# Splitting two weight blocks at a time in a two-layer hybrid transformer

## The chip, the cores and the metric

The kernel runs on one core of a Trainium2 chip. The core has a matrix engine (TensorE, PE in the profile), a vector engine (VectorE, DVE), a scalar engine (ScalarE, ACT), GpSimd (POOL) and a queue engine (SyncE, SP) that issues most of the loads. The metric is the time of one execution on the device in microseconds, as the median of several runs.

## The reference

The input is 512 tokens of width 1024 and a memory of 256 rows. There are two layers. Each one normalises its input, mixes tokens, projects with `w_out`, and adds a normalised result to the residual; then it runs a gated feed-forward of hidden width 2816. Layer 0 mixes with a chunked spatial gate, layer 1 with causal attention that has a forget gate; both also attend to the memory with four heads. Cut to what matters:

```python
for layer in range(DEPTH):
    a = rmsnorm(h, ln_mix_pre[layer])
    main = chunked_spatial_gating(...) if layer == 0 else forgetting_attention(...)
    mixed = jnp.concatenate([main, memory_attention(q_mem, mem_n, w_mem_kv[layer])], axis=-1)
    h = h + rmsnorm(mixed @ w_out[layer], ln_mix_post[layer])
    f = rmsnorm(h, ln_ffn_pre[layer])
    f = (jax.nn.silu(f @ w_ffn_gate[layer]) * (f @ w_ffn_up[layer])) @ w_ffn_down[layer]
    h = h + rmsnorm(f, ln_ffn_post[layer])
```

All inputs and outputs are float32.

## The kernel before

**Products in parts.** Each float32 operand is split into a high part, rounded to the format `fp32r`, and a low part, the remainder. A product is then three matmuls: high by high, high by low and low by high (`mm3`, lines 189 to 193). The split (`split`, line 238) is one cast on ScalarE, which makes the high part, and one subtraction on VectorE, which makes the low part; both stand in the profile under L239. Weights arrive by a load of 128 x 1024 float32 (512 KB) into a tile named `raw`, of which there are four, and are split in two halves of 128 x 512. The parts lie in tiles named `whi` and `wlo`, from two rings of eight tiles each (`pair_of_parts`, line 131). `prepared` (line 147) and `moving_pair` (line 164) load and split; with `aside` they put the parts elsewhere, among the activations.

**Feed-forward.** It takes most of the time (about 206 to 490 us for layer 0 and 780 to 1060 us for layer 1). Two hidden blocks of 128 columns are made at a time for the gate, and two for the up projection, by a scheme that replaces eight quadrant products by seven. The class `Seven` (line 1018) does this: its two raw tiles hold the quadrants a11, a12 and a21, a22, each 128 x 512. `sums` (line 1037) forms four combinations on VectorE (lines 1041, 1043, 1045, 1046), and `run` (line 1052) does one product: 12 matmuls of 128 columns of weights by 256 tokens. Products are numbered 1 to 7 and each needs one split quadrant or combination: 1 needs a11, 2 needs a12, 7 needs the combination s3, and 6, 3, 5 and 4 need what the sums have left in a11, a12, a21 and a22. Products 1, 6 and 5 share one bank, 7 and 4 another, and 2 and 3 write the two halves of a third. ScalarE copies a bank between two products that are not to be added. `sevens` (line 1088) calls them in the order 1, 7, 2, 6, 4, 3, 5, apart from the first pair of a layer, which runs 1, 2, 3 for gate and up, then (7, 6) and (4, 5) for each.

The 22 hidden blocks are worked in an opening pair and five groups of four (`groups`, line 1120). A group has four Sevens, two for the gate and two for the up projection. After each of the first four groups comes `down_sevens` (line 1238): the down projection by a seven-product scheme of its own (class `DownSeven`, line 1185) with 128 x 512 quadrants, two blocks together. There the banks of the output are `yc`, `ys` and `yl`. The hidden activations are combined and split by `Inner` (line 1158).

**Attention.** In layer 1 the heads run one after another, and the projections of keys, values and outputs are cut into pieces that are put between the steps of the heads (`attend`, line 539; `queue`, line 214). `pair_split` (line 1483) splits queries and keys of two heads.

**Order.** The program names each operation's engine. The Tile framework then orders the instructions of each engine by priority and by its own estimate of costs, gives each tile a place in its ring, and lets a place go when the last reader of the tile is done. Each engine works in its order; loads of weights wait in SP's queue until a raw tile is free.

Of the kernel before, what the change touches and what calls it, by code (L numbers as in the profile page):

```python
# [15 lines left out]
P = 128  # L16
# [24 lines left out]
def hybrid(ctx: ExitStack, tc: tile.TileContext, i: dict, out: bass.AP):  # L41
# [113 lines left out]
    def weight_parts(raw, shape, aside=False):  # L155
        n = shape[0] * shape[1]
        parts = []
        for d in range(0, n, 512):
            pair = pair_of_parts(min(512, n - d), aside)
            split(raw[:, d : min(d + 512, n)], *pair)  # L160
            parts += cut(pair, shape[1])
        return parts

    def moving_pair(src, aside=False):

        raw = wp.tile([P, 1024], F32, tag="raw", name=name("raw"), bufs=4)
        last_load[0] = nc.sync.dma_start(raw.rearrange("p (m c) -> p m c", m=4), src)
        four = raw.rearrange("p (m k c) -> p m k c", m=4, k=2)
        parts = []
        for x in range(2):  # L170
            hi, lo = (t.rearrange("p (m c) -> p m c", m=4) for t in pair_of_parts(aside=aside))
            split(four[:, :, x, :], hi, lo)
            parts.append((hi, lo))
        return parts
# [415 lines left out]
    def layer_a():  # L590
# [3 lines left out]
        wq, raws = ([], []), [wp.tile([P, 1024], F32, tag="raw", name=name("raw"), bufs=4) for _ in range(2)]  # L594

        def query_weights(m, c0, c1):
# [49 lines left out]
        with tc.tile_pool(name="sgu", bufs=1) as lp:  # L646
# [126 lines left out]
            stats()  # L773
            ws = []
            for n in range(3):
                both = wp.tile([P, 536], F32R, tag=("hi", "lo")[n % 2], name=name("ws"), bufs=8)[:, :512].rearrange(
                    "p (g x c) -> p g x c", g=2, x=2)
                split(wsf[:, 256 * n : 256 * n + 256].rearrange("p (g c) -> p g c", g=2), both[:, :, 0, :], both[:, :, 1, :])
                ws += [both[:, g, :, :] for g in range(2)]
# [238 lines left out]
    class Seven:  # L1018
# [5 lines left out]
        def __init__(self, xs, src, tag, rows):  # L1024
            self.xs, self.rows = xs, rows
            w1, w2 = loaded(src(0)), loaded(src(1))
            self.a = [w[:, d : d + 512] for w in (w1, w2) for d in (0, 512)]
            self.x, self.p = ps(tag, s="x"), ps(tag, (P, 256), s="a")
            self.q = ps(tag, (P, 256), s="e")
            self.s1, self.s2 = prob("s1"), prob("s2")  # L1030

        def parts(self, src):
            pair = pair_of_parts()
            split(src, *pair)
            return pair

        def sums(self):

            a11, a12, a21, a22 = self.a
# [5 lines left out]
            V.tensor_add(a11, a21, a11)  # L1045
            V.tensor_add(a12, a11, a12)

        def product(self, o, w, n, more=False):
# [3 lines left out]
        def run(self, what):  # L1052

            a11, a12, a21, a22 = self.a
            left, right = (slice(*c) for c in HALVES)
            s1, s2 = self.s1, self.s2
            if what == 1:
                self.product(self.p, self.w1, 0)
                A.copy(s1[:, left], self.p)
            elif what == 2:  # L1060
                self.product(self.x[:, left], self.w2, 2)
            elif what == 3:
                self.product(self.x[:, right], self.parts(a12), 5)
            elif what == 4:
                self.product(self.q, self.parts(a22), 4, True)
            elif what == 5:
                self.product(self.p, self.parts(a21), 6, True)
                A.copy(s1[:, right], self.p)
            elif what == 6:
                self.product(self.p, self.parts(a11), 3, True)  # L1070
                A.copy(s2[:, left], self.p)
            else:
                self.product(self.q, self.parts(self.s3), 1)
                A.copy(s2[:, right], self.q)
# [13 lines left out]
    def sevens(pair, plain_first, opens=False, rest=None):  # L1088

        if not plain_first:  # L1090
            for make in pair:
                u = make()
                with behind(ended if opens else ()):
                    u.sums()
                opens = False
                for n in (1, 7, 2, 6, 4, 3, 5):
                    u.run(n)
                    if rest and n == 2:
                        rest()
                        rest = None  # L1100
                u.end()
            return
# [13 lines left out]
    def feed_forward(layer, phase, xp, meanwhile=None):  # L1116
# [68 lines left out]
        class DownSeven:  # L1185

            def __init__(self, k, spare):
                if spare:
# [25 lines left out]
            def parts(self, src, aside=False):  # L1214
                pair = pair_of_parts()
                split_aside(src, *(t.rearrange("p (m c) -> p m c", m=4) for t in pair), aside)
                return pair
# [95 lines left out]
        for gi, (k0, k1) in enumerate(groups):  # L1313
            fs, pairs, downs = [], [], []
            for m in range(k0, k1, 2):
                if meanwhile and m == k1 - 2 and gi == len(groups) - 1:
                    next(meanwhile)
                if gi < len(groups) - 1:
                    pairs.append(Inner(m < k1 - 2))
                    if m > k0:  # L1320
                        downs.append(DownSeven(m, True))
                else:
# [5 lines left out]
            if gi == len(groups) - 1:  # L1328
# [3 lines left out]
                if meanwhile:  # L1332
# [7 lines left out]
                               layer == 1)  # L1340
            rest = down_sevens([DownSeven(k0, False)] + downs, pairs)


    def layer_b(phase, fp):
# [62 lines left out]
        def value_block(j):  # L1407
# [4 lines left out]
            def load():  # L1412
                for kh in range(2):
# [3 lines left out]
                    raw = loaded(i["w_v"][j, kh]).rearrange("p (a b) -> p a b", b=256)  # L1417
                    for x in range(0, 4, 2):
                        pair = [t.rearrange("p (a b) -> p a b", a=2) for t in pair_of_parts(2 * width)]
                        k = 4 * kh + x  # L1420
                        split(raw[:, x : x + 2, :], *(t[:, :, :256] for t in pair))
                        split(wf[:, k : k + 2, :], *(t[:, :, 256:] for t in pair))
                        w.extend(tuple(t[:, y, :] for t in pair) for y in range(2))

# [217 lines left out]
```

## Time and profile before

| what | value |
|---|---|
| median of 3 runs | 1090.25 us (1089.44 to 1091.18) |
| profiled execution | 1089.34 us |
| its span, first to last instruction | 1087.6 us |
| mean granted TensorE clock | 0.999 |
| TensorE busy | 1079.2 us, 7266 matmuls |
| weight loads busy (PEld) | 982.4 us |
| VectorE busy | 971.8 us, 1942 instructions |
| ScalarE busy | 755.9 us, 1588 instructions |
| GpSimd busy | 93.5 us, 120 instructions |

A row of a group names the line, the engine, the operation, the tiles (out<-in) and the shapes, then the count, the busy time in us and the mean of one in ns, and after the second bar the idle time before them and what ended it. A row of a wait reads "engine tile line <- releaser: us in total, times, longest". A row of the timeline has the start and the length in us. Matmuls overlap, so their rows are longer than the distance between two starts.

### The profile page before, as it was taken

The page shows a single profiled execution, that of the slowest core. Times are in us where ns is not written, and L with a number is a line of the kernel's source. Part 1 is how long each engine was busy: PE and PEld are TensorE (multiplying, and loading weights), DVE is VectorE, ACT ScalarE, POOL GpSimd, SP SyncE. Part 2 cuts the span into 40 slices and gives each one's busy share as a digit, 9 for nine tenths or more (in the row PEclk, how much of TensorE's full clock was granted, in tenths as well). Part 3 has the DMA queues.
Part 4 walks back from the last instruction along what each step waited for, and adds up shares of the span by engine and source line. Part 5 has one row for each costly group of instructions (what it writes and reads, how often), then busy time and mean ns, then how long its engine had stood idle before and what let it go on. Part 6 is the DMA issues. An engine that isn't in the chain of part 4 may idle for free.

```text
span 1087.6 us, 19810 instructions
## 1 busy us (share of the span) xinstructions
PE 1079.2 (99%) x7266; PEld 982.4 (90%) x7267; DVE 971.8 (89%) x1942; ACT 755.9 (69%) x1588; POOL 93.5 (9%) x120
## 2 busy tenths in 40 slices
PE   9999999999999999999999999999999999999998
PEld 8998889998989898998988998889997989898996
DVE  7879768999999999997968789868999999999986
ACT  7776578667766667577747788868666666757664
POOL 1000000002020202001000000000002010201100
PEclk9999999999999999999999999999999999999999
DMA  7421441338464664746222654531347465564632
GB/s 272 161 83 42 121 130 39 117 97 194 128 156 129 144 182 97 195 145 187 78 78 61 156 135 125 151 117 40 99 116 173 119 154 158 120 193 94 177 97 78
DMA packets 83993, 139.65 MB, mean 128 GB/s; under 512 B 6772, under 2 KB 49800, under 8 KB 83896
## 3 DMA queue, kind: packets, MB, share of 16 engines
q1 hardware_dynamic: 71480, 116.57, 34.9%
q0 software_dynamic: 11712, 21.50, 11.6%
q8 instruction: 57, 0.93, 0.4%
q10 hardware_dynamic: 704, 0.32, 0.1%
q14 instruction: 40, 0.33, 0.1%
HBM read 105.23 MB, written 2.10 MB: 99 GB/s over the span
## 4 chain that ended last, share of the span: by engine, by line
PE 71%; DVE 19%; DMA 4%; issue 3%; ACT 3%; SPq 0%; DVEq 0%; ACTq 0%
DVE wlo L239 6%; PE y L191 5%; PE y L192 5%; PE y L193 5%; PE ps L191 4%; PE ps L193 4%; PE ps L192 4%; DMA raw<-in_w_gate 4%; PE a L191 3%; PE a L192 3%; PE a L193 2%; PE v L191 2%; PE yc L191 2%; PE v L192 2%; PE v L193 2%
## 5 line engine op out<-in xcount | busy, mean ns | idle before, releaser
L239 ACT CAST whi<-raw 128x512 fp32r<-128x512 f32 x444 | 264.0, 620 | 100.7 <-DVE raw L1045 27.4
L239 DVE TENSOR_TENSOR wlo<-raw,whi 128x512 fp32r<-128x512 f32 x444 | 292.5, 687 | 22.1 <-ACT whi L239 21.2
L191 PE MATMUL x<-xshi,whi 128*128 128x256 f32 x320 | 90.0, 281 | 0.0
L193 PE MATMUL x<-xshi,wlo 128*128 128x256 f32 x320 | 90.0, 281 | 0.0
L191 PE MATMUL a<-xshi,whi 128*128 128x256 f32 x320 | 90.0, 281 | 0.0
L192 PE MATMUL x<-xslo,whi 128*128 128x256 f32 x320 | 89.9, 281 | 0.0
L192 PE MATMUL a<-xslo,whi 128*128 128x256 f32 x320 | 89.8, 281 | 0.0
L193 PE MATMUL a<-xshi,wlo 128*128 128x256 f32 x320 | 89.8, 281 | 0.0
L191 PE MATMUL ps<-xshi,whi 128*128 128x256 f32 (+1 forms) x224 | 68.5, 306 | 0.0
L192 PE MATMUL ps<-xslo,whi 128*128 128x256 f32 (+1 forms) x224 | 66.7, 298 | 0.0
L193 PE MATMUL ps<-xshi,wlo 128*128 128x256 f32 (+1 forms) x224 | 66.4, 298 | 0.0
L239 ACT CAST whi<-s 128x512 fp32r<-128x512 f32 x56 | 34.8, 621 | 38.8 <-DVE s L1208 18.6
L192 PEld LDWEIGHTS a<-xslo,whi 128*128 128x128 f32 x320 | 60.3, 189 | 0.4
L191 PEld LDWEIGHTS a<-xshi,whi 128*128 128x128 f32 x320 | 60.3, 188 | 0.4
L193 PEld LDWEIGHTS x<-xshi,wlo 128*128 128x128 f32 x320 | 60.4, 189 | 0.0
L192 PEld LDWEIGHTS x<-xslo,whi 128*128 128x128 f32 x320 | 60.3, 189 | 0.0
L193 PEld LDWEIGHTS a<-xshi,wlo 128*128 128x128 f32 x320 | 60.3, 189 | 0.0
L191 PEld LDWEIGHTS x<-xshi,whi 128*128 128x128 f32 x320 | 60.3, 188 | 0.0
L1243 POOL DMA_DIRECT2D y<-yo x48 | 41.4, 953 | 192.2 <-ACT yo L1242 130.8
L191 PE MATMUL y<-whi,mixedhi 128*128 128x512 f32 x128 | 51.4, 401 | 0.0
L192 PE MATMUL y<-wlo,mixedhi 128*128 128x512 f32 x128 | 50.7, 396 | 0.0
L193 PE MATMUL y<-whi,mixedlo 128*128 128x512 f32 x128 | 50.4, 394 | 0.0
(353 smaller groups left out, 3656.3 us busy)
## 6 DMA issues: line engine op xcount, KB each, us to landing
raw<-in_w_gate SPq DMA_DIRECT2D x44, 512.0 KB, 4.5
raw<-in_w_up SPq DMA_DIRECT2D x44, 512.0 KB, 5.7
y<-yo POOLq DMA_DIRECT2D x64, 256.0 KB, 4.9
raw<-in_w_down SPq DMA_DIRECT2D x28, 512.0 KB, 4.1
raw<-in_w_out SPq DMA_DIRECT2D x16, 512.0 KB, 4.0
wd<-in_w_down SPq DMA_DIRECT2D x32, 256.0 KB
flo<-s POOLq DMA_DIRECT2D x16, 256.0 KB, 4.8
raw<-in_w_b_q SPq DMA_DIRECT2D x8, 512.0 KB, 4.4
```

The costliest lines, as they stand in the source:

```text
L191: PE.matmul(o, w[0], x[0], start=start, stop=False, skip_group_check=more)
L192: PE.matmul(o, w[0], x[1], start=False, stop=False, skip_group_check=more)
L193: return PE.matmul(o, w[1], x[0], start=False, stop=stop, skip_group_check=more)
L239: last_parts[:] = A.copy(hi, src), (eng or V).tensor_sub(lo, src, hi)
L1243: G.dma_start(ys[to[0]][to[1]], some, accum_op=ALU.add)
```

## The change

Two neighbouring blocks of 512 columns are cast and subtracted together, as one of 1024, and the rings have four tiles of 1072 columns where they had eight of 512 (536 for one block). `prepared` and `moving_pair` split a whole raw tile at once. In `Seven`, the quadrants are split as (1, 2), (6, 3), (5, 4) and 7 alone, and the order of the products becomes 1, 2, 7, 6, 3, 4, 5, which puts the two halves of each wide tile next to each other; the pair (6, 3) is split when the first of its products is due. Where two blocks are not neighbours, only the tile is shared and the splits stay 512 wide: the query weights of layer 0, the quadrants of the down products (through the new class `Halves`), and queries and keys in `pair_split`. The spatial weights of layer 0 take three halves of one pair of wide tiles.

```diff
-    def pair_of_parts(n=512, aside=False):
-        if aside:
-            return act("whi"), act("wlo")
-        return (wp.tile([P, max(n, 512)], F32R, tag="hi", name=name("whi"), bufs=8)[:, :n],
-                wp.tile([P, max(n, 512)], F32R, tag="lo", name=name("wlo"), bufs=8)[:, :n])
+    def pair_of_parts(n=1024):
+        return tuple(wp.tile([P, 1072], F32R, tag=t, name=name("w" + t), bufs=4)[:, :n] for t in ("hi", "lo"))
+
+    class Halves:
+
+        def __init__(self):
+            self.left = []
+
+        def __call__(self):
+            if not self.left:
+                self.left = cut(pair_of_parts(), 512)
+            return self.left.pop(0)
...
     def weight_parts(raw, shape, aside=False):
         n = shape[0] * shape[1]
+        step = 512 if aside else n
         parts = []
-        for d in range(0, n, 512):
-            pair = pair_of_parts(min(512, n - d), aside)
-            split(raw[:, d : min(d + 512, n)], *pair)
+        for d in range(0, n, step):
+            pair = (act("whi"), act("wlo")) if aside else pair_of_parts(n)
+            split(raw[:, d : d + step], *pair)
             parts += cut(pair, shape[1])
         return parts
...
+        if not aside:
+            pair = pair_of_parts()
+            split(raw, *pair)
+            hi, lo = (t.rearrange("p (m k c) -> p m k c", m=4, k=2) for t in pair)
+            return [(hi[:, :, x, :], lo[:, :, x, :]) for x in range(2)]
...
-        def parts(self, src):
-            pair = pair_of_parts()
-            split(src, *pair)
-            return pair
+        def parts(self, *ns):
+            pair = pair_of_parts(512 * len(ns))
+            split(self.raw[ns], *pair)
+            self.w.update(zip(ns, cut(pair, 512)))
 
         def sums(self):
 
             a11, a12, a21, a22 = self.a
-            self.s3 = temp("s3")
-            V.tensor_add(self.s3, a11, a21)
-            self.w1 = self.parts(a11)
+            s3 = temp("s3")
+            self.w, self.raw = {}, {(1, 2): self.raws[0], (6, 3): self.raws[0], (5, 4): self.raws[1], (7,): s3}
+            V.tensor_add(s3, a11, a21)
+            self.parts(1, 2)
             V.tensor_add(a21, a21, a22)
-            self.w2 = self.parts(a12)
             V.tensor_add(a11, a21, a11)
             V.tensor_add(a12, a11, a12)
+
+        def weights(self, n):
+            if n not in self.w:
+                self.parts(*next(ns for ns in self.raw if n in ns))
+            return self.w[n]
...
-                for n in (1, 7, 2, 6, 4, 3, 5):
+                for n in (1, 2, 7, 6, 3, 4, 5):
                     u.run(n)
-                    if rest and n == 2:
+                    if rest and n == 7:
...
             def parts(self, src, aside=False):
-                pair = pair_of_parts()
+                pair = self.halves()
...
-            pair["q"], pair["k"] = pair_of_parts(), pair_of_parts()
+            pair["q"], pair["k"] = cut(pair_of_parts(), 512)
```

More of the change, by code (lines that the diff above doesn't have):

```diff
@@ L168, in moving_pair @@
         four = raw.rearrange("p (m k c) -> p m k c", m=4, k=2)
+        if not aside:
[3 more added lines that the diff above has]
+            return [(hi[:, :, x, :], lo[:, :, x, :]) for x in range(2)]
         parts = []
         for x in range(2):
-            hi, lo = (t.rearrange("p (m c) -> p m c", m=4) for t in pair_of_parts(aside=aside))
+            hi, lo = (act(t).rearrange("p (m c) -> p m c", m=4) for t in ("whi", "wlo"))
             split(four[:, :, x, :], hi, lo)
@@ L594, in layer_a @@
         wq, raws = ([], []), [wp.tile([P, 1024], F32, tag="raw", name=name("raw"), bufs=4) for _ in range(2)]
+        query_parts = [pair_of_parts() for _ in range(2)]
         def query_weights(m, c0, c1):
@@ L598, in query_weights @@
             for c in range(c0, c1, 512):
-                pair = pair_of_parts()
+                pair = tuple(t[:, c : c + 512] for t in query_parts[m])
                 split(raws[m][:, c : c + 512], *pair)
@@ L774, in layer_a @@
             ws = []
+            hi, lo = pair_of_parts()
+            room = hi[:, :512], lo[:, :512], hi[:, 512:]
             for n in range(3):
-                both = wp.tile([P, 536], F32R, tag=("hi", "lo")[n % 2], name=name("ws"), bufs=8)[:, :512].rearrange(
-                    "p (g x c) -> p g x c", g=2, x=2)
+                both = room[n].rearrange("p (g x c) -> p g x c", g=2, x=2)
                 split(wsf[:, 256 * n : 256 * n + 256].rearrange("p (g c) -> p g c", g=2), both[:, :, 0, :], both[:, :, 1, :])
@@ L1052, in run @@
         def run(self, what):
-            a11, a12, a21, a22 = self.a
             left, right = (slice(*c) for c in HALVES)
@@ L1057, in run @@
             if what == 1:
-                self.product(self.p, self.w1, 0)
+                self.product(self.p, self.weights(1), 0)
                 A.copy(s1[:, left], self.p)
             elif what == 2:
-                self.product(self.x[:, left], self.w2, 2)
+                self.product(self.x[:, left], self.weights(2), 2)
             elif what == 3:
-                self.product(self.x[:, right], self.parts(a12), 5)
+                self.product(self.x[:, right], self.weights(3), 5)
             elif what == 4:
-                self.product(self.q, self.parts(a22), 4, True)
+                self.product(self.q, self.weights(4), 4, True)
             elif what == 5:
-                self.product(self.p, self.parts(a21), 6, True)
+                self.product(self.p, self.weights(5), 6, True)
                 A.copy(s1[:, right], self.p)
             elif what == 6:
-                self.product(self.p, self.parts(a11), 3, True)
+                self.product(self.p, self.weights(6), 3, True)
                 A.copy(s2[:, left], self.p)
             else:
-                self.product(self.q, self.parts(self.s3), 1)
+                self.product(self.q, self.weights(7), 1)
                 A.copy(s2[:, right], self.q)
@@ L1185, in feed_forward, with __init__ @@
         class DownSeven:
-            def __init__(self, k, spare):
+            def __init__(self, k, spare, halves):
+                self.halves = halves
                 if spare:
@@ L1313, in feed_forward @@
         for gi, (k0, k1) in enumerate(groups):
-            fs, pairs, downs = [], [], []
+            fs, pairs, downs, halves = [], [], [], Halves()
             for m in range(k0, k1, 2):
@@ L1320, in feed_forward @@
                     if m > k0:
-                        downs.append(DownSeven(m, True))
+                        downs.append(DownSeven(m, True, halves))
                 else:
@@ L1417, in load @@
                     raw = loaded(i["w_v"][j, kh]).rearrange("p (a b) -> p a b", b=256)
[L1418 to L1423, printed above, removed]
+                    pair = [t.rearrange("p (a b) -> p a b", a=4) for t in pair_of_parts(4 * width)]
+                    split(raw, *(t[:, :, :256] for t in pair))
+                    split(wf[:, 4 * kh : 4 * kh + 4, :], *(t[:, :, 256:] for t in pair))
+                    w.extend(tuple(t[:, y, :] for t in pair) for y in range(4))
             def piece(tk, kh):
```

6 lines of the change are left out of this document (3 added, 3 removed).

## The prediction

> **What bounds the kernel now.** I began with the profile's page: the busy time of each engine, and the forty slices.
>
> ```profile
> span 1087.6 us, 19810 instructions
> PE 1079.2 (99%) x7266; PEld 982.4 (90%) x7267; DVE 971.8 (89%) x1942; ACT 755.9 (69%) x1588; POOL 93.5 (9%) x120
> DVE  7879768999999999997968789868999999999986
> PEclk9999999999999999999999999999999999999999
> ```
>
> TensorE is busy in 1079.2 of 1087.6 us and its clock is never lowered. VectorE stands at 90% or more in two long blocks of slices, which are the two feed-forward layers. The next view is the busy time by stage: the feed-forward of layer 0 with its four down products, a stretch of three Sevens alone, the attention of layer 1, and the feed-forward of layer 1. Columns: length, then PE, PEld, DVE, ACT and POOL busy with their instruction counts, the granted clock, the DMA share and GB/s.
>
> ```profile
> 206.00:441.00 235.00, 234.29 (x1641) 216.12 (x1640) 231.24 (x414) 159.54 (x319) 33.22 (x38) 1.00 0.58 146
> 441.90:471.70 29.80, 29.80 (x252) 29.75 (x251) 29.77 (x55) 19.19 (x42) 1.72 (x2) 1.00 0.53 156
> 580.00:720.00 140.00, 139.36 (x836) 120.54 (x835) 116.51 (x317) 111.17 (x273) 0.00 (x0) 1.00 0.48 125
> 780.00:1011.00 231.00, 229.69 (x1622) 212.22 (x1621) 227.97 (x408) 157.14 (x316) 32.79 (x38) 1.00 0.57 143
> ```
>
> In the three Sevens, TensorE starts 252 matmuls in 29.80 us, one every 0.118 us without a hole, while VectorE is just as full: 29.77 of 29.80 us. Both are full at once, so I have to find out which one makes the other wait. The lead tells it: the part that product 7 reads, and the moment at which product 7 reads it.
>
> ```profile
> 448.98 0.69 DVE L239 TENSOR_TENSOR wlo<-s,whi 128x512 fp32r<-128x512 f32 x1
> 453.50 0.28 PE L191 MATMUL e<-t3hi,whi 128*128 128x256 f32 x1
> ```
>
> The low part is done at 448.98 + 0.69 = 449.67, and product 7 starts at 453.50: 3.8 us ahead, or 2.7 products (a product is 12 matmuls, 12 x 0.118 = 1.42 us). So TensorE sets the pace inside the Sevens and VectorE keeps up with some stock. Where does TensorE wait at all? First the list of its waits over the whole run, then the eight stretches in which the down products of a group run.
>
> ```profile
> PE idle L89 <- DVE zeros L81: 1.3, 1, 1.3
> PE ys L193 <- DVE flo L239: 0.6, 3, 0.2
> PE yc L191 <- ACT yo L1242: 0.5, 3, 0.2
> PE ys L191 <- DVE s L1080: 0.4, 1, 0.4
> 241.40:262.48 21.08, 20.73 (x86) 1.00 0.65 134
> 302.26:322.33 20.07, 19.98 (x86) 1.00 0.67 137
> 362.06:382.09 20.03, 19.96 (x87) 1.00 0.66 136
> 421.98:442.13 20.15, 19.95 (x86) 1.00 0.66 140
> 815.09:836.58 21.49, 20.78 (x87) 1.00 0.64 131
> 876.29:896.36 20.07, 19.96 (x86) 1.00 0.67 137
> 936.02:956.15 20.13, 19.98 (x86) 1.00 0.68 139
> 995.83:1016.30 20.47, 20.14 (x87) 1.00 0.61 128
> ```
>
> The waits shown are tiny, but a matmul row is longer than the distance between two starts, so a late start hides under the end of the one before. The starts themselves say more:
>
> ```profile
> 818.54 0.40 PE L191 MATMUL yl<-whi,fhi 128*128 128x512 f32 x1
> 819.70 0.40 PE L193 MATMUL yl<-whi,flo 128*128 128x512 f32 x1
> 816.97 0.39 PE L193 MATMUL ys<-whi,flo 128*128 128x512 f32 x1
> 817.74 0.50 PE L191 MATMUL ys<-whi,fhi 128*128 128x512 f32 x1 [0.38 <-DVE s L1080]
> 824.22 0.40 PE L192 MATMUL ys<-wlo,fhi 128*128 128x512 f32 x1
> 824.85 0.50 PE L193 MATMUL ys<-whi,flo 128*128 128x512 f32 x1 [0.23 <-DVE flo L239]
> ```
>
> From 818.54 to 819.70 lie five steps, 0.232 us each. A down stretch is 7 products x 2 blocks x 2 token blocks x 3 = 84 matmuls, 84 x 0.232 = 19.49 us (the counts of 86 and 87 take in neighbours that overlap the edges). The eight stretches sum to 163.49 us, their floor to 155.92: 7.6 us are lost there, and hardly anything in the Sevens. The two starts shown are 0.77 - 0.23 = 0.54 and 0.63 - 0.23 = 0.40 us late, both behind VectorE. Those 7.6 us are the most that these stretches can give back.
>
> **The change, part by part.** *Merged splits.* A split is one ACT cast and one DVE subtraction. The groups of the splits, and the same operations at half the width, priced by form:
>
> ```profile
> L239 DVE TENSOR_TENSOR wlo<-raw,whi 128x512 fp32r<-128x512 f32 x444 | 292.5, 687 | 22.1 <-ACT whi L239 21.2
> L239 ACT CAST whi<-raw 128x512 fp32r<-128x512 f32 x444 | 264.0, 620 | 100.7 <-DVE raw L1045 27.4 <-PE a L192 24.6 <-PE ps L192 14.8
> L239 DVE TENSOR_TENSOR b<-s,b 128x256 fp32r<-128x256 f32 x16 | 6.8, 422 | 0.2 <-ACT b L239 0.2
> L239 ACT CAST b<-s 128x256 fp32r<-128x256 f32 x16 | 6.5, 405 | 0.6 <-ACT fhi L239 0.3
> 450.51 2.49 DVE L239 TENSOR_TENSOR wlo<-raw,whi 128x512 fp32r<-128x512 f32 x4
> 449.10 1.14 ACT L239 CAST whi<-raw 128x512 fp32r<-128x512 f32 x2 [0.71 <-DVE raw L1045]
> ```
>
> No row shows a split of 1024, so I carry the line on. DVE: 256 more elements cost 687 - 422 = 265 ns, so 1024 take 687 + 530 = 1217 ns. Four in a row took 2.49 us, so starts are (2.49 - 0.69) / 3 = 0.60 us apart and 87 ns of each overlap the next. A merged subtraction occupies 1217 - 87 = 1130 ns where two occupied 1200: 70 ns less. The bounds are 0 (no fixed part) and 157 ns (687 - 530, all of the fixed part); I take 70, because the spacing is what a full engine feels. ACT: 620 - 405 = 215 per 256, so 1050 ns; spacing 1.14 - 0.62 = 0.52; merged 950 against 1040: 90 ns less, bounds 0 and 190.
>
> How many? Each of the 40 Sevens goes from 7 splits to 4, so 120 merges. The other 62 are counted in the code: memory keys and values 8, first projection 12, first blocks of the three boundaries 6, first down weights 4, output weights 8, unaside tail weights 8, layer-1 queries 4, keys 6, values 6. The small forget columns merge twice more. The three kinds that only share a tile (query weights, q/k pair, down quadrants through Halves) keep 512-wide splits. VectorE loses 182 x 70 ns = 12.7 us of work, ScalarE 182 x 90 ns = 16.4 us. Inside the Sevens all of it lies beside matmuls that start every 0.118 us anyway: cost and gain there are 0. Were that cover gone, a Seven would gain 3 x 70 = 0.21 us of its 9.93.
>
> *What reaches the end.* A group has four Sevens, 12 merges, 0.84 us less VectorE work before its down products. The waits behind VectorE at these stretches (the low part of the hidden activations, and the sums of line 1080) should shrink by up to that. From the two starts above, 0.54 + 0.40 us, and the smaller late starts in the other six (those six lose 0.54 to 0.98 us each, of which the copies of the chain banks by ACT, line 1242, take about half), I put the part owed to VectorE at 2.5 us of the 7.6. The chain-bank copies wait for TensorE itself and stay. Bounds 0 and 7.6; I take 1.5, the row of the three visible low-part waits being nearest: **-1.5 us**.
>
> *Later first use.* The first product of a pair now waits for a cast and a subtraction of double width: 1050 - 620 + 1217 - 687 = 0.96 us later if both start when they did. The 3.8 us of lead hide that; where no lead is left it costs up to 0.96 us each time.
>
> *The order 1, 2, 7, 6, 3, 4, 5.* It lets the halves of a pair be used one behind the other. Product 2 writes a bank of its own; 7 still has 6 and 3 between it and the product 4 that adds to its bank, 6 has 2 and 7 between it and product 1. So no product moves closer to the copy that empties its bank than two products, 2.8 us against copies of 0.36 us: 0. The cast of (6, 3) has to wait for both sums, lines 1045 and 1046, not for the first alone; they precede product 6 by a product and more: 0. The raw tiles are let go after the subtractions of (6, 3) and (5, 4); SP's loads are queued behind that, and the first of the two is earlier than before, where product 3 split last but one: 0, bounds -0.3 and +0.3 us per layer.
>
> *Four slots of 1072 for eight of 512.* Bytes are the same, but a slot is let go only when both halves are read. The rows of ACT waiting for a slot, and of the loads behind the splits:
>
> ```profile
> ACT whi L239 <- PE a L192: 24.6, 40, 0.8
> SPq L144 <- DVE wlo L239: 256.2, 66, 27.1
> ```
>
> Already one cast per Seven (40 times, 0.6 us on average) waits until TensorE has read an old high part, so the ring is full once a Seven. With four slots TensorE holds one pair and five products' worth can lie ready: 5 x 1.42 = 7.1 us between a slot's release and its next need, against 1.05 + 1.22 = 2.3 us to fill it, plus what stands ahead on VectorE. That hides it: 0; the price without this cover is in the rivals.
>
> *Attention of layer 1.* 32 of its splits become 16:
>
> ```profile
> L239 DVE TENSOR_TENSOR wlo<-raw,whi 128x512 fp32r<-128x512 f32 x32 | 21.5, 685 | 1.9 <-ACT whi L239 1.7
> ```
>
> VectorE is busy in 116.51 of 140 us there and ScalarE in 111.17, so nothing is gained by less work as such; a softmax step that finds a merged subtraction ahead of it can be 0.53 us later. Bounds: 16 x 0.07 = -1.1 and 16 x 0.53 = +8.5 us. Projection matmuls stand ready to fill such holes (TensorE shows 0.64 us idle in 140), so I take **+0.3 us**.
>
> The sum goes against the profiled execution's own time, 1089.34 us, which is 1.74 over its span: 1089.34 - 1.5 + 0.3 = 1088.1. That execution lies 0.9 below the median of the runs, 1090.25, so the forecast for the median is **1089.0 us**: no change that can be told from none, 0.2% (2.2 us) being about what a measurement of this kernel tells.
>
> **The rivals.** *A: VectorE's relief goes further.* If its lag at the end of each group is what holds the down stretches, half or more of the 7.6 us goes: 1090.25 - 4 = 1086.2, with everything 1082.7. For it: both stretches with the most loss (21.08, 21.49) follow the first groups, where VectorE must also finish the inputs. Against it: five of eight lose only 0.5 to 0.7 us.
>
> *B: the coarser ring makes TensorE wait (slower).* Place: where a group's down products begin. Slots there are shared between the last pair of the Sevens and the first two down quadrants, and one tile holds the quadrants 1 and 7, taken long before 7 is multiplied. If a free slot appears one product late, filling it takes 2.3 us and the product in hand covers 1.4: 0.9 us per stretch, 8 x 0.9 = 7.2, less the 1.5: 1090.25 + 5.7 = 1096. It decides once VectorE's lead there is under about 1 us. For it: ACT's 40 waits on the ring. Against it: they are at most 0.8 us and TensorE never waited in answer.
> The Trainium skill, Perfetto Trace Analysis, section Identifying Performance Opportunities, says that the same gap repeating on the engine that should be saturated can mean that there was no room for the next tile; this trace has such a gap on ACT (24.6 us in 40), not on TensorE.
>
> *C: long instructions stand in the way in attention (slower).* If a third of the 16 merged subtractions hold back a step that TensorE needs, 5.3 x 0.53 = 2.8 us: 1090.25 + 2.8 = 1093. For it: neither VectorE (83%) nor ScalarE (79%) is full there. Against it: the 0.64 us of idle.
> The Trainium skill, Perfetto Trace Analysis, section Optimizing Scalar/DVE Operations, recommends grouping where such an engine is saturated, and breaking instructions up where it isn't but makes others wait; by that rule the change is right in the Sevens and wrong here.
>
> **How the numbers follow.** Forecast 0.47, A 0.28, B 0.12, C 0.13. The forecast's own range is 1087.7 to 1091.5, so a little of it falls under 1088.07: faster 0.30, same 0.45, slower 0.25. The range runs from 1085.5 (most of A) to 1094.0 (all of C, little of B), which also holds the -1.1 of attention with half of A.
>
> **What would show it.** Right: merged casts near 1050 and subtractions near 1217 ns, 182 of each; VectorE's busy time down by 12 to 19 us with TensorE's start spacing still 0.118; the two longest down stretches below 20.7 us. Wrong: waits of TensorE behind the low parts inside the Sevens (B), a down stretch above 21.5, or more than 0.64 us of TensorE idle between 580 and 720 (C).

## The result and the profile after

The changed kernel takes 1105.17 us, the median of six runs (1100.90 to 1108.80); the kernel before, run beside it, takes 1090.61 us (1089.44 to 1091.53). The ratio is 1.0135, with a 95% interval of 1.0110 to 1.0161. The change makes the kernel **slower by 14.6 us**. The forecast was 1089.0 us and the range ended at 1094.0, so the forecast and its range were wrong.

The page of the changed kernel, its span and the engines' busy time. The profiled execution took 1104.32 us:

```profile
span 1102.6 us, 19371 instructions
PE 1081.0 (98%) x7266; PEld 979.1 (89%) x7267; DVE 963.1 (87%) x1758; ACT 734.4 (67%) x1404; POOL 93.8 (9%) x120
```

TensorE has the same 7266 matmuls, at the same clock (0.999). VectorE has lost 8.7 us of work and ScalarE 21.5 us, as the change means them to. The span has grown by 15.0 us all the same. Where do they lie? The eight stretches of the down products, with the same columns as in the prediction:

```profile
244.21:264.70 20.49, 19.99 (x86) 1.00 0.61 123
304.61:326.72 22.11, 20.61 (x86) 1.00 0.62 127
366.06:388.21 22.15, 20.64 (x87) 1.00 0.62 128
427.70:449.29 21.59, 20.66 (x86) 1.00 0.61 129
827.96:848.45 20.49, 19.98 (x86) 1.00 0.61 125
...
sum 171.35, PE 163.66; mean PE 20.46
```

They sum to 171.35 us where they were 163.49: 7.9 us more. The change isn't even. The first stretch of each layer became shorter (21.08 to 20.49 and 21.49 to 20.49, 1.6 us together), and the other six grew by 9.5 us. Line numbers have moved: the split, L239 before, is L252; the first and last sums of a Seven, L1041 and L1046, are L1059 and L1063; the sum L1080 at the end of a Seven is L1101.

To place the rest I took all starts of TensorE in the trace and summed by how much each is late, that is, the distance from the start before it less 0.117 us (256 columns) or 0.230 us (512):

| late starts of TensorE, us | before | after |
|---|---|---|
| Sevens of each layer's first group | 0.8 | 5.5 |
| Sevens of layer 0's last group | 0.4 | 2.4 |
| Sevens of the other groups | 2.9 | 1.4 |
| down products | 8.8 | 16.8 |
| everything else, attention included | 30.6 | 32.2 |

So 13.2 of the 15 us are lost in the feed-forwards, at three places: in the first group of a layer, in the last group of layer 0, and where a group's down products run. The 1.5 us by which the other Sevens differ are 0.6 ns on each of their 2352 starts: in the Sevens of the kernel before no single start is over 0.02 us late, so this is a spacing and not a wait that went away. Why TensorE is late at the three places begins on VectorE. Groups of VectorE and ScalarE instructions, by form:

```profile
L252 DVE TENSOR_TENSOR wlo<-raw,whi 128x1024 fp32r<-128x1024 f32 x182 | 219.3, 1219 | 17.4 <-ACT whi L252 17.0
L252 ACT CAST whi<-raw 128x1024 fp32r<-128x1024 f32 x182 | 189.5, 1048 | 128.2 <-DVE raw L1063 57.7 <-PE x L205 19.2 <-issue 9.7
L1059 DVE TENSOR_TENSOR s<-raw,raw 128x512 f32<-128x512 f32 x40 | 27.4, 686 | 16.6 <-DMA raw<-in_w_gate 15.7 <-DMA raw<-in_w_up 0.8
```

The merged instructions cost what was forecast. But the first sum of a Seven now finds VectorE idle for 16.6 us in all, because its quadrants have not been loaded; before, it was 1.7 us. One such case, followed through the timeline of the changed kernel (start, length, instruction, and in brackets the idle time before it and what ended it):

```profile
264.88 2.00 ACT L252 CAST whi<-raw 128x1024 fp32r<-128x1024 f32 x2 [3.98 <-PE yc L206]
266.51 2.35 DVE L252 TENSOR_TENSOR wlo<-raw,whi 128x1024 fp32r<-128x1024 f32 x2
267.75 1.47 SPq L151 DMA_DIRECT2D raw<-in_w_gate  x2
272.43 0.69 DVE L1063 TENSOR_TENSOR raw<-raw 128x512 f32<-128x512 f32 x1
275.48 0.69 DVE L1059 TENSOR_TENSOR s<-raw,raw 128x512 f32<-128x512 f32 x1 [2.36 <-DMA raw<-in_w_gate]
...
307.47 0.41 DVE L1101 TENSOR_TENSOR s<-a,s 128x256 f32<-128x256 f32 x1
306.48 0.40 PE L206 MATMUL ys<-whi,flo 128*128 128x512 f32 x1
307.94 0.50 PE L204 MATMUL ys<-whi,fhi 128*128 128x512 f32 x1 [1.06 <-DVE s L1101]
```

Read it from the top. ScalarE waits 3.98 us for a place for the parts, until a down product (`yc`) has let one go. The two wide casts then run, the two wide subtractions end at 267.73 and 268.86, and each time SP can issue a load into the raw tile that is free at last. The second of these loads lands some 6.6 us after its issue. VectorE, which works in its fixed order, runs out of work at 273.12 and stands idle until 275.48. From there to 307.88 no idle time is shown on it; the sum at 307.47, which frees a bank for `ys`, comes at the end of that unbroken row, and TensorE's next matmul starts 307.94 - 306.48 - 0.23 = 1.2 us late behind it. That the hole is what made the sum late is read from this order; the runs below put it to the test. The same happens at 213.86, where the hole is 2.61 us long and VectorE then has none until product 6 stalls:

```profile
213.86 0.69 DVE L1059 TENSOR_TENSOR s<-raw,raw 128x512 f32<-128x512 f32 x1 [2.61 <-DMA raw<-in_w_gate]
...
235.90 0.68 DVE L1063 TENSOR_TENSOR raw<-raw 128x512 f32<-128x512 f32 x1
236.61 1.04 ACT L252 CAST whi<-raw 128x1024 fp32r<-128x1024 f32 x1
236.39 0.28 PE L206 MATMUL e<-t3hi,wlo 128*128 128x256 f32 x1
237.71 0.39 PE L204 MATMUL a<-d2hi,whi 128*128 128x256 f32 x1 [1.03 <-ACT whi L252]
```

The last sum of that Seven ends at 236.58, the wide cast of (6, 3) starts at 236.61, and product 6, which could have started at 236.51, starts at 237.71. The twin of this start in layer 1, at 821.43, is 1.27 us late.

The casts show what holds the parts back. First the waits of ScalarE in the kernel before, then after (in all, times, longest):

```profile
ACT whi L239 <- DVE raw L1045: 27.4, 27, 1.8
ACT whi L239 <- PE a L192: 24.6, 40, 0.8
ACT whi L239 <- PE x L192: 6.6, 13, 0.6
```

```profile
ACT whi L252 <- DVE raw L1063: 57.7, 27, 3.5
ACT whi L252 <- PE x L205: 19.6, 24, 1.0
ACT whi L252 <- PE a L205: 11.0, 14, 1.3
ACT whi L252 <- PE yc L206: 8.0, 2, 4.0
```

The wait for the sums has doubled. The waits for a place (those on PE) are fewer but longer: up to 4.0 us, where in the feed-forwards none was above 0.8.

### The profile page after: what moved, and what is told of

Same layout as the page of the kernel before. It is cut to its first block, busy times and chain, and to the rows that moved or that the text cites. A ratio compares the mean times of both kernels' runs of the same rounds, so it can differ in the third digit from the quotient of the medians.

```text
span 1102.6 us, 19371 instructions
## 1 busy us (share of the span) xinstructions
PE 1081.0 (98%) x7266; PEld 979.1 (89%) x7267; DVE 963.1 (87%) x1758; ACT 734.4 (67%) x1404; POOL 93.8 (9%) x120
## 4 chain that ended last, share of the span: by engine, by line
PE 67%; DVE 22%; ACT 4%; issue 3%; DMA 3%; SPq 0%; DVEq 0%; ACTq 0%
DVE wlo L252 8%; PE y L205 4%; PE y L206 4%; PE y L204 4%; PE ps L204 4%; PE ps L206 4%; PE ps L205 4%; DMA raw<-in_w_gate 2%; PE a L204 2%; PE a L205 2%; PE a L206 2%; PE v L204 2%; PE v L206 2%; PE v L205 2%; PE yc L204 2%
## 5 line engine op out<-in xcount | busy, mean ns | idle before, releaser
L252 ACT CAST whi<-raw 128x1024 fp32r<-128x1024 f32 (+1 forms) x262 | 237.2, 917 | 138.1 <-DVE raw L1063 57.7
L252 DVE TENSOR_TENSOR wlo<-raw,whi 128x1024 fp32r<-128x1024 f32 (+1 forms) x262 | 272.8, 1056 | 22.6 <-ACT whi L252 21.9
L204 PE MATMUL a<-d2hi,whi 128*128 128x256 f32 x160 | 45.3, 283 | 2.1 <-ACT whi L252 2.1
```

Source lines behind the costliest of these rows:

```text
L204: PE.matmul(o, w[0], x[0], start=start, stop=False, skip_group_check=more)
L252: last_parts[:] = A.copy(hi, src), (eng or V).tensor_sub(lo, src, hi)
```

## The experiments

Two theories ran against each other. The **places**: four wide places for the parts are fewer and coarser than eight narrow ones, so casts wait for a place. The **merged splits**: a wide cast of (6, 3) waits for the last sum, and a raw tile is let go only after a wide subtraction, so sums, loads and the work behind them come late. Beside them stood the **order** of the products. Every kernel computes the whole reference. "Idle behind loads" is VectorE's idle time before the first sums; "FFN late" is the sum of late starts in Sevens and down products, 12.9 us before and 26.1 after.

### The order of the products alone

The kernel before, with the new order and nothing else:

```diff
-                for n in (1, 7, 2, 6, 4, 3, 5):
+                for n in (1, 2, 7, 6, 3, 4, 5):
-                    if rest and n == 2:
+                    if rest and n == 7:
```

> The kernel before with nothing but the order of the products changed to 1, 2, 7, 6, 3, 4, 5; 512-wide splits, rings of eight. Both theories: the order by itself is neutral, 1088 to 1093. A third theory, that the order is what hurts: 1098 or more.

Measured: 1092.63 us, 1.0023 (1.0013 to 1.0034). FFN late is 15.3 us and idle behind loads 5.6 us. The order costs about 2.5 us, a sixth of the loss.

### Fewer narrow places

The kernel before, with its two rings cut from eight tiles to seven and to six:

```diff
-        return (wp.tile([P, max(n, 512)], F32R, tag="hi", name=name("whi"), bufs=8)[:, :n],
-                wp.tile([P, max(n, 512)], F32R, tag="lo", name=name("wlo"), bufs=8)[:, :n])
+        return (wp.tile([P, max(n, 512)], F32R, tag="hi", name=name("whi"), bufs=6)[:, :n],
+                wp.tile([P, max(n, 512)], F32R, tag="lo", name=name("wlo"), bufs=6)[:, :n])
```

> The kernel before, with rings of seven tiles of 512 in place of eight; nothing else. In the wide ring of the changed kernel a Seven's four tiles hold 7 x 512 useful columns, since product 7 fills half of one. Theory 2 (too few places for parts): 1094 to 1105, TensorE late at the down products as in the changed kernel. Theory 1 (the merged split itself): one place less is nothing, 1089 to 1092.

> The kernel before, with rings of six tiles of 512. Theory 2: more than with seven, 1100 to 1115; a wide slot is let go one product (1.4 us) later than a narrow one, which is about another place. Theory 1: 1089 to 1094.

Measured: 1093.09 us with seven (1.0033; 1.0020 to 1.0046), between the two theories' ranges, and 1100.53 us with six (1.0100; 1.0084 to 1.0116), in the range of the places. A wait of ScalarE with six:

```profile
ACT whi L239 <- PE a L192: 39.6, 62, 2.0
```

62 waits up to 2.0 us where there were 40 up to 0.8. Losing two narrow places costs 10.9 us with nothing else changed: the ring had almost no stock to give away. FFN late goes from 12.9 to 25.0 us, above all in the down products (8.8 to 17.1), as in the changed kernel (16.8).

### The merged splits undone, in the changed kernel

`halves` keeps the wide tiles and splits each half of a Seven's pair when its product is due. `apart63` does that for (6, 3) alone.

```diff
-        def parts(self, *ns):
-            pair = pair_of_parts(512 * len(ns))
-            split(self.raw[ns], *pair)
-            self.w.update(zip(ns, cut(pair, 512)))
+        def parts(self, n):
+            ns = next(ns for ns in self.raw if n in ns)
+            if n not in self.room:
+                pair = pair_of_parts(512 * len(ns))
+                self.room.update(zip(ns, cut(pair, 512)))
+                if ns not in ((1, 2), (6, 3), (5, 4)):
+                    split(self.raw[ns], *pair)
+                    self.w.update(zip(ns, cut(pair, 512)))
+            if n not in self.w:
+                at = 512 * ns.index(n)
+                split(self.raw[ns][:, at : at + 512], *self.room[n])
+                self.w[n] = self.room[n]
```

> The changed kernel, but in the Sevens each product's 512 columns are cast and subtracted by themselves when that product is due, into the wide tiles; new order, ring of four and the merged splits outside the Sevens stay. Theory 1 (the merged split is what hurts: the cast of (6, 3) has to wait for the last of the three sums, and raw tiles are let go late behind that): 1090 to 1093 us, VectorE idle at the first sum behind loads down from 16.6 us to under 5. Theory 2 (the ring of four wide tiles is what hurts, a slot being let go only when both halves are read): stays at 1101 to 1109, with the same idle time behind loads.

> The changed kernel, but of the Seven's pairs only (6, 3) is split in two halves of 512, each when its product is due; (1, 2) and (5, 4) stay merged. Theory 1, in its narrow form (the wait of one cast for both sums): most of the 14.6 us comes back, 1091 to 1095, and the late starts of product 6 behind ScalarE's cast (1.2 us each) are gone. Theory 2: no change, 1101 to 1109.

Measured: `halves` 1102.59 us (1.0108; 1.0087 to 1.0129), `apart63` 1106.92 us (1.0151; 1.0132 to 1.0171). In `halves` the wait for the last sums shrinks, and the wait for a place grows:

```profile
ACT whi L252 <- PE x L205: 36.4, 38, 1.0
ACT whi L252 <- PE a L205: 16.0, 15, 2.0
ACT whi L252 <- DVE raw L1072: 12.0, 23, 2.0
```

On four wide places the merged splits are therefore not what costs the 14.6 us: without them 12.5 remain. Splitting (6, 3) alone gains nothing.

The kernel to set beside `halves` is the one with the order alone. Both split each half of a pair by itself, in the same order of products, so they differ by the wide places and by the wide splits outside the Sevens: 1092.63 to 1102.59 us, 10.0 us, and FFN late goes from 15.3 to 24.1 us.

### The sums first

The changed kernel, with its three in-place sums at high priority:

```diff
+            with tc.high_priority():
-            V.tensor_add(a21, a21, a22)
-            V.tensor_add(a11, a21, a11)
-            V.tensor_add(a12, a11, a12)
+                V.tensor_add(a21, a21, a22)
+                V.tensor_add(a11, a21, a11)
+                V.tensor_add(a12, a11, a12)
```

> The changed kernel, with the three sums in the raw tiles raised in priority, so that VectorE does them as soon as their operands are there; splits, ring and order stay. Theory 1: the cast of (6, 3) and the raw tiles come earlier and half or more of the loss goes, 1092 to 1098. Theory 2: 1101 to 1109, as the slots are no freer.

Measured: 1101.11 us (1.0101; 1.0086 to 1.0116), about 4 us better than the change; idle behind loads stays at 15.5 us. Late sums alone are not the cause.

### The pairing without the wide tiles

The kernel before with the new order, its eight narrow places and its 512-wide splits, but both halves of a pair split together when the first is due:

```diff
+        def weights(self, n):
+            if n not in self.w:
+                ns = next(ns for ns in self.src if n in ns)
+                self.w.update(zip(ns, [self.parts(src) for src in self.src[ns]]))
+            return self.w[n]
```

> The kernel before in the new order, with narrow tiles, rings of eight and 512-wide splits, but both splits of a pair, (1, 2), (6, 3) and (5, 4), are called together when the first of them is due. If it is the pairing that hurts (two places claimed at once, the raw tile let go later, both sums needed first): 1097 or more, and VectorE idle at the first sum behind loads above 10 us. If pairing costs nothing with narrow tiles: 1091 to 1094, as with the order alone, and what hurts is the width of the instruction and of the place.

Measured: 1096.12 us (1.0061; 1.0046 to 1.0076), 3.5 us over the order alone and between the two ranges. ScalarE's wait for the sums is as long as in the changed kernel:

```profile
ACT whi L239 <- DVE raw L1045: 56.4, 34, 2.4
```

but with eight narrow places it costs little. The kernels so far take 1090.6 us before, 1092.6 with the order, 1096.1 with the pairs split together in narrow tiles, 1102.6 in `halves` and 1105.2 with everything. These are not the steps of one stair, as `halves` has the wide places but takes the pairing back.

### Product 7 in tiles of its own

The changed kernel, where product 7's parts don't take half a wide place but a pair of 512-wide tiles of their own (one pair). To make room, the masks and the small forget tiles move to the pool of layer 1's attention. `own7_sums` adds the high priority for the sums.

```diff
-            pair = pair_of_parts(512 * len(ns))
+            pair = pair_of_parts(1024) if len(ns) > 1 else tuple(
+                seven_pool[0].tile([P, T], F32R, tag=f"w7{t}", name=name("w" + t), bufs=1) for t in ("hi", "lo"))
```

> The changed kernel, but the parts of product 7 lie in a pair of 512-wide tiles of their own, so that the four wide slots serve only the pairs (1, 2), (6, 3), (5, 4) and the down quadrants. To make room, the masks and small tiles of layer 1's attention are kept in that layer's own pool. Theory 2: a third or more of a slot's time is free again, and most of the loss goes, 1091 to 1097. Theory 1: 1100 to 1107 as before, with product 6 still late behind its cast.

> As the kernel with product 7's parts in tiles of their own, and the three sums raised in priority. If both causes add: 1088 to 1093, and less than with either alone. If only the ring counts: the same as with the tiles alone.

Measured: 1115.92 us (1.0241; 1.0224 to 1.0259) and 1115.76 us (1.0237; 1.0221 to 1.0252): both worse than the change, a miss. A new wait of TensorE appears in the first of them:

```profile
PE e L212 <- ACT s L1105: 5.5, 5, 1.6
```

Product 4 waits for ScalarE to empty its bank. But moving the masks is an edit too (the next control), so this pair doesn't separate the theories.

### Five wide places, and the splits merged or not

Five places need room. The rings go into pools that live for one stage (4 x 1072 outside the feed-forwards), and small tiles move out. So there is a control, `ring4s`, with the same pools and four wide places of 1024 in the feed-forwards. Four kernels make a square: four or five places, merged or halved splits (halved as in `halves`).

```diff
+    with tc.tile_pool(name="ffn0", bufs=4) as xp, ring_of("ring_f0", 1024, 4):
...
-    with tc.tile_pool(name="ffn0", bufs=4) as xp, ring_of("ring_f0", 1024, 4):
+    with tc.tile_pool(name="ffn0", bufs=4) as xp, ring_of("ring_f0", 1024, 5):
...
-    last_ring = ctx.enter_context(ring_of("ring_f1", 1024, 4))
+    last_ring = ctx.enter_context(ring_of("ring_f1", 1024, 5))
```

> A control: the changed kernel with its wide rings in pools that live for one stage each (four places of 1024 in the feed-forwards, four of 1072 elsewhere), and with the masks and small tiles of layer 1 in that layer's pool. Nothing in the feed-forward's work differs. Every theory: 1100 to 1110, as the changed kernel; anything else is the price of moving tiles.

> As the control, with five wide places in the feed-forwards in place of four; all splits merged as in the changed kernel. Theory 2 (too few places): most of the loss goes, 1090 to 1096. Theory 1 (the merged split delays the first half and the raw tiles): 1100 or more.

> Five wide places, and in the Sevens 512-wide splits, each when its product is due. Theory 2: 1090 to 1094, no better than with merged splits. If the ring and the merged split both cost: this is the one near 1091, and the merged one with five places lies between.

> The control with pools of one stage, four wide places, and 512-wide splits in the Sevens. With five places the same kernel took 1098.1 and its late starts in the feed-forwards were those of the kernel before. If the fifth place is what did that: 1106 to 1110 here, with late starts in Sevens and down products together near 24 us. If the 512-wide splits did it alone: 1097 to 1100.

Measured, in us, with the ratio to the kernel before and its interval, and FFN late:

| | splits merged | splits halved |
|---|---|---|
| four places | 1112.27, 1.0213 (1.0196 to 1.0230), late 28.0 | 1114.02, 1.0217 (1.0200 to 1.0234), late 27.9 |
| five places | 1113.42, 1.0218 (1.0178 to 1.0258), late 26.9 | 1098.10, 1.0077 (1.0062 to 1.0092), late 13.0 |

Either remedy alone gives nothing; both together give 14 to 16 us, and bring FFN late to 13.0 us, where the kernel before has 12.9. With the fifth place alone the late starts only move, from the Sevens (15.1 to 10.5 us) to the down products (12.9 to 16.4). The casts' waits shift too. Four places merged, five places merged, four places halved, five places halved (L1081 and L1090 are the last sums, L1089 the one before):

```profile
ACT whi L269 <- DVE raw L1081: 55.7, 26, 3.4
ACT whi L269 <- PE x L222: 22.8, 27, 1.0
ACT whi L269 <- PE a L222: 18.4, 22, 1.7
```

```profile
ACT whi L269 <- DVE raw L1081: 72.5, 29, 3.9
ACT whi L269 <- PE x L222: 7.3, 9, 1.0
```

```profile
ACT whi L269 <- PE x L222: 37.6, 39, 1.0
ACT whi L269 <- PE a L222: 27.0, 22, 2.0
ACT whi L269 <- DVE raw L1090: 9.3, 22, 0.9
```

```profile
ACT whi L269 <- DVE raw L1089: 26.3, 23, 2.1
ACT whi L269 <- PE a L222: 19.0, 20, 1.2
ACT whi L269 <- PE x L222: 18.4, 25, 1.0
```

A fifth place takes most of the waits for a place away, and the wait for the sums rises to 72.5 us. Halved splits take the wait for the sums away, and those for a place rise. Only with both does the kernel come back to about the waits of the kernel before. There VectorE never waits for a load, and the down stretches are shorter than ever:

```profile
L1085 DVE TENSOR_TENSOR s<-raw,raw 128x512 f32<-128x512 f32 x40 | 27.5, 688 | 0.0
```

```profile
sum 161.26, PE 160.73; mean PE 20.09
```

161.26 us against 163.49 before. This kernel is still slower than the one before, because its late starts outside the feed-forwards are 40.1 us, like those of its control (38.2), and not 30.6.

### Five raw tiles, and the sums first on five places

`raw5s` is the control with a fifth raw tile in the feed-forwards; for that its raw tiles, too, lie in pools that live for one stage. `ring5_sums` is `ring5` with the sums at high priority (that diff stands above).

```diff
-    with tc.tile_pool(name="ffn0", bufs=4) as xp, ring_of("ring_f0", 1024, 4):
+    with tc.tile_pool(name="ffn0", bufs=4) as xp, ring_of("ring_f0", 1024, 4, 5):
```

> The control with five raw tiles in the feed-forwards in place of four, and four wide places. If the loss comes from VectorE idling at the first sum behind late loads (16.6 us of idle in the changed kernel): 1092 to 1098. If the places for parts are what runs out: 1099 or more, with the idle at the first sum gone all the same.

> Five wide places, merged splits, and the three sums raised in priority. If with five places the merged split hurts because its cast waits for sums that VectorE does late: 1100 to 1106, late starts near 15 us. If it hurts because raw tiles, and with them the loads and the first sum, come late: 1110 or more, with VectorE still idle some 15 to 20 us at the first sum.

Measured: `raw5s` 1123.37 us (1.0306; 1.0291 to 1.0322), `ring5_sums` 1115.34 us (1.0223; 1.0199 to 1.0248). With the fifth raw tile VectorE's idle time behind loads falls from 15.7 to 1.3 us:

```profile
L1077 DVE TENSOR_TENSOR s<-raw,raw 128x512 f32<-128x512 f32 x40 | 27.5, 688 | 1.3 <-DMA raw<-in_w_up 0.7 <-DMA raw<-in_w_gate 0.5
```

FFN late falls only from 28.0 to 21.5 us: a load that comes late accounts for a part, and the rest stays. It is the Sevens that gain (15.1 to 8.8 us). The down products stay at 12.9 and 12.7; only the two late starts behind the sum that frees `ys`, 1.1 us together in the control, are gone. The time as a whole gets worse because the late starts outside the feed-forwards rise to 55.0 us. The trace shows where: at each change of stage. One of three:

```profile
506.94 0.38 SPq L192 DMA_DIRECT2D raw<-in_w_down  x1
512.07 0.79 PE L221 MATMUL y<-whi,fhi 128*128 128x512 f32 x1 [5.17 <-ACT whi L269]
```

The last matmul of the stage before ends at 506.91, SP then issues the first load into the new stage's raw tiles, and TensorE starts again 5.3 us late, when that block has come and been split. The other two, at 146.49 and 741.57, are 4.9 us late each. The control is 4.0 us late at these three starts, so they make 11.1 of the 16.8 us by which 55.0 exceeds its 38.2. So this run prices the late loads in the feed-forwards, but its total says nothing about a fifth raw tile as such.

Putting the sums first doesn't help on five places either, where idle behind loads is 23.0 us.

## Why the prediction was wrong

**Prices: right.** 182 merged subtractions of 1219 ns and 182 casts of 1048 ns were measured where 1217 and 1050 were forecast. TensorE's spacing is unchanged. VectorE's busy time fell by 8.7 us, below the 12 to 19 named as the sign: 48 ns per merge where 70 were taken, inside the bounds of 0 and 157. Back to back, two wide subtractions start 2.35 - 1.22 = 1.13 us apart, which is the forecast spacing. ScalarE's busy time fell by 21.5 us, 118 ns per merge where 90 were taken.

**"-1.5 us" at the down stretches: wrong in sign.** They grew by 7.9 us. The two longest did fall below 20.7 us, which was named as a sign of being right, and the 1.6 us are what the term forecast; but both follow the first groups, where TensorE had by then lost 2.3 and 2.4 us more than before, so VectorE may only have caught up. The other six grew, four of them past the 21.5 named as a sign of being wrong. The Trainium skill, Perfetto Trace Analysis, section Optimizing Scalar/DVE Operations, says that grouping can improve throughput where such an engine is saturated. VectorE was that in the Sevens, and the grouping did lower its work, but it had idle time behind loads (16.6 us in all) where it had little before, and no throughput was gained: in the steady Sevens TensorE set the pace already.

**"Four slots of 1072 for eight of 512: 0": wrong, the first of two main errors.** The argument counted products' worth of parts in a steady Seven. It didn't count the transitions, where a place holds a last pair, a single product 7 in half a place, or two down quadrants used far apart. Cutting the narrow ring to six shows that two places less cost 10.9 us, so the 40 waits of ScalarE were the sign of a ring that was just large enough; wide places with narrow splits in the Sevens (`halves` against the order alone) cost 10.0 us. Rival B named the ring and the place, with a chance of only 0.12, because it was argued that TensorE had never waited in answer. That its 7.2 us lie near the 7.9 by which the down stretches grew is luck: it had 0.9 us in each of the eight, and measured are -1.0 to +2.1. And B let TensorE wait for parts, while the largest of its waits there is for the sum that frees a bank of `ys` (3.9 us in 5 cases). The Trainium skill, Perfetto Trace Analysis, section Identifying Performance Opportunities, has the rule cited there, that a repeating gap on the engine that should be saturated can mean that there is no room for the next tile. Here the gap lay on ScalarE, of which the rule doesn't speak; the run with six places shows that it meant a full ring all the same.

**"They precede product 6 by a product and more: 0" and "raw tiles: 0, bounds ±0.3": wrong, the second.** The wide cast of (6, 3) waited 57.7 us in 27 cases for the last sum, and product 6 started 1.2 us late in the case shown. The two wide subtractions let raw tiles go late; the 6.6 us of the load then left VectorE idle 16.6 us in all. The prediction had SP's long waits behind the splits before it (256.2 us) and put the release at nothing, because in the new order the first of the two comes earlier. In the kernel before the loads came just in time: VectorE's idle time before the first sums was 1.7 us. It didn't ask what a later release would do.

**Each of these two causes is enough by itself.** In the square, removing one leaves the loss whole. That is why no single undoing, `halves` included, brought the time back. The square stands on the control with the moved tiles; that the same holds without them is inferred from the like sizes (FFN late 26.1 and 28.0 us with everything, 24.1 and 27.9 halved).

**"3.8 us ahead": measured in the wrong place.** The lead was read in the second Seven of layer 0's last group, and in that Seven it held. But two Sevens later, in the same group of the kernel before, the low part of product 7 is done at 472.75 and product 7 starts at 473.38, 0.6 us behind it; in the changed kernel product 7 waits there for its low part and is 1.8 us late:

```profile
472.06 0.69 DVE L239 TENSOR_TENSOR wlo<-s,whi 128x512 fp32r<-128x512 f32 x1
473.38 0.28 PE L191 MATMUL e<-t3hi,whi 128*128 128x256 f32 x1
```

```profile
483.91 0.39 PE L206 MATMUL e<-t3hi,wlo 128*128 128x256 f32 x1 [1.64 <-DVE wlo L252]
```

Of the 40 Sevens before, three have a lead of 1.1 us or less at product 7: this one, and the last of each layer's first group (1.1 and 0.7 us). These are the three in which the changed kernel loses over 1 us at one start (483.91, 237.71, 821.43). The prediction's own term said that a start can be up to 0.96 us later "where no lead is left", and counted no such place.

**The order, "0": wrong by 2.5 us.** FFN late rises by 2.4 us with the order alone. Whether the two products of distance to the bank copies were too few, or VectorE's work was merely placed less well, the run doesn't tell.

**Attention, "+0.3": small, as forecast.**

```profile
585.00:725.00 140.00, 138.39 (x847) 120.82 (x846) 114.74 (x305) 107.82 (x256) 0.00 (x0) 1.00 0.47 122
```

TensorE is idle 1.61 us in about the stretch of the attention, 0.64 before. That is the sign named for rival C, with 1.0 us where C had 2.8. All late starts outside the feed-forwards grew by 1.6 us. Rival A is refuted as a whole: VectorE has less work, and at most the two longest down stretches have anything from it.

**What stays open.** Five wide places without moved tiles were not tried, as there is no room for them, so how much of the 14.6 us each cause has can't be given as two numbers. Pairing the splits costs 3.5 us with eight narrow places and merging them 15 us with five wide ones; whether the width of the instruction or that of the place makes the difference, no run separates. Each edit also lets the framework order the instructions anew; differences of 2 or 3 us between two of these kernels can be that, and the reasons given for them are argued, not shown. What the square and the ring of six show is far larger than that.

## What to carry to other kernels

Merging two instructions also merges their waits and their releases: the result is ready only when the later input is, and both the source and the place are held until the later reader is done. Before merging, look at the waits of the engines that aren't the bottleneck: here ScalarE's 40 waits for a place and loads that landed just as they were needed meant that there was no stock, and a saving of 0.07 us each didn't pay for that. Measure the lead in every repeat, and take the smallest: it lies at the transitions between kinds of work, not in the steady part. And when two causes can each hold the loss, undo both at once before ruling one out.

## What the runs showed that was not expected

Moving small tiles and the rings into pools of one stage, with four places as before (1024 columns wide instead of 1072 in the feed-forwards), costs 7 us (`ring4s` 1112.27 against 1105.17). Most of the late starts that it adds lie outside the feed-forwards (32.2 to 38.2 us), and 4.0 us of these are two starts at a change of stage, at 506.06 and 731.66, late by 1.7 and 2.4 us behind the first cast into the new stage's ring; the weights are made ready there only after the border, while in the changed kernel no start of `y` is over 0.25 us late. `raw5s`, whose raw tiles lie in such pools too, removes the wait that it was meant to remove and is 11 us slower than its control. And the changed kernel's runs spread over 0.7% (1100.90 to 1108.80), where those of the kernel before lie within 0.2%; no run explains that.
